# One fixed place for the high and low parts of all seven-block weight chunks

## The chip, the cores and the metric

The kernel runs on one core of a Trainium2 chip. The metric is the device time of one execution in microseconds; the kernel before takes 1150.22 us, the median of three runs from 1149.85 to 1150.63.

## The reference

A two-layer encoder trunk over 512 tokens of 1024 features, in float32. Each layer is attention followed by a squared-ReLU MLP, both with a residual sum. The part that matters here is the MLP, whose two weight matrices are 1024 x 4096 and 4096 x 1024:

```python
def sq_relu_mlp(h, w_up, w_down):
    u = jax.nn.relu(h @ w_up)
    return (u * u) @ w_down

h = h + sq_relu_mlp(rmsnorm(h, norm_ffn[layer]), ffn_w_up[layer], ffn_w_down[layer])
```

## The kernel before

All activations are held transposed, features on the 128 partitions and tokens along the free dimension. A float32 product is made of three TensorE matmuls on rounded parts: high weights by high activations, high weights by low activations, low weights by high activations. The weight part is the stationary operand (128 x 128, loaded by a weight load that the profile calls PEld), the activation part is the moving one.

Most of the two MLP products go through a seven-multiplication scheme for 2 x 2 blocks (class Seven). There a **seven-block chunk** is a 256 x 256 piece of the weight matrix. Four of its 128 x 128 blocks are loaded by one DMA on SP's queue (line 367), three sums of blocks are made beside them in place (lines 372 to 374, on POOL, or on DVE for a few chunks of the down product), and the seven blocks that are needed lie then in columns 128 to 1023 of a 1024-column tile, 896 columns in all. ACT copies these 896 columns into a rounded high part (tile whi, line 379) and DVE subtracts that from the source into a low part (tile wlo, line 380).

In Seven.run, TensorE takes a chunk's seven blocks one after the other; for each block it does three matmuls with 256 moving columns (lines 467, 468 and 469): high part by x[:, 0], high part by x[:, 1], low part by x[:, 0]. That is 21 matmuls and 21 weight loads a chunk. Four chunks and more accumulate in half banks of PSUM, which ACT and DVE then add up (lines 475 to 479). The moving tiles are those of pool "big" (Slot, named a), 1024 columns of 4 bytes, and what is read of them starts at column 0, 256, 512 or 768.

There are 164 such chunks, in four stretches: 52 in the up product of the first layer, 32 in its down product, and 52 and 28 in the second layer. Between the stretches TensorE does the rest of the products with 512 moving columns (lines 623 to 625, function mm3), attention and norms.

Buffers: three tiles for high parts, four for low parts, four raw tiles, beside which a chunk's raw data goes into a slot of the big pool where enough are free. A planner that runs ahead of the products (weights, begin, preload) sets the order: DMAs five chunks ahead, sums up to three, the copy and the subtraction two.

All these tiles (a, whi, wlo, raw) have 1024 columns, that is 4096 bytes in each partition, and in the built program each of them begins at the same remainder modulo 256 bytes. So the column at which a part begins inside its whi or wlo tile, modulo 64, says how far it stands from the moving tiles modulo 256 bytes. In the kernel before, places() chooses that column anew for each chunk: chunk i has its high part at column 8 * (i mod 16) and its low part at that place moved on by a table's entry for i div 16, again modulo 128 columns.

```python
a = i % 16
return 8 * a, 8 * ((a + (0, 1, 2, 4, 8, 3, 6, 12, 15, 14)[i // 16 % 10]) % 16)
```

Of the kernel before, what the change touches and what calls it, by code (L numbers as in the profile page):

```python
# [9 lines left out]
F32R = mybir.dt.float32r  # L10
# [8 lines left out]
P = 128  # L19
# [11 lines left out]
def f32(ap):  # L31
    return ap.bitcast(F32)
# [3 lines left out]
def encoder_kernel(ctx: ExitStack, tc: tile.TileContext, ins, out, dbg=None):  # L36
# [5 lines left out]
    wp = ctx.enter_context(tc.tile_pool(name="wp", bufs=3))  # L42
# [19 lines left out]
    def nm(s):  # L62
        cnt[0] += 1
        return f"{s}_{cnt[0]}"
# [204 lines left out]
    def rows(w, k0, nk):  # L269
        return w[k0 * P : (k0 + nk) * P, :].rearrange("(k p) n -> p k n", p=P)  # L270
# [16 lines left out]
    def begin(i):  # L287
        while begun[0] < len(loaded):
            make = asked[begun[0]][0]
            if make is summed_chunk and begun[0] > i + SUM:  # L290
                break
            if make in (summed_chunk, seven_chunk):
                next(loaded[begun[0]])
            begun[0] += 1
# [55 lines left out]
    SEVEN = [(0, 0), (2, 2), (4, 5), (3, 3), (5, 4), (6, 1), (1, 6)]  # L350

    reserve = [3]
    place = [0]

    def places():

        i = place[0]
        place[0] += 1
        a = i % 16
        return 8 * a, 8 * ((a + (0, 1, 2, 4, 8, 3, 6, 12, 15, 14)[i // 16 % 10]) % 16)  # L360

    def seven_chunk(w, k0, c0, eng=None):


        slot = Slot(F32) if len(free) > reserve[0] else None
        raw = slot.t if slot else wp.tile([P, 1024], F32, tag="raw", bufs=4, name=nm("raw"))
        SP.dma_start(raw[:, 0:512].rearrange("p (k n) -> p k n", k=2), rows(w, k0, 2)[:, :, c0 : c0 + 256])
        r = raw.rearrange("p (b n) -> p b n", n=P)
        yield
        held = (lambda z: z) if eng else tc.keep_in_program_order  # L370
        eng = eng or POOL
        held(eng.tensor_tensor(r[:, 6], r[:, 0], r[:, 1], op=ALU.subtract))  # L372
        held(eng.tensor_tensor(r[:, 4:6], r[:, 2:3].to_broadcast([P, 2, P]), r[:, 0:7:6], op=ALU.add))  # L373
        held(eng.tensor_tensor(r[:, 7], r[:, 3], r[:, 5], op=ALU.subtract))  # L374
        yield
        a, b = places()
        hi = wp.tile([P, 1024], F32R, tag="whi", name=nm("whi"))[:, a : a + 896]
        lo = wp.tile([P, 1024], F32R, tag="wlo", bufs=4, name=nm("wlo"))[:, b : b + 896]
        ACT.activation(hi, raw[:, 128:1024], AF.Copy)  # L379
        DVE.tensor_tensor(lo, raw[:, 128:1024], f32(hi), op=ALU.subtract)  # L380
        if slot:
            slot.free()
        yield hi, lo, []

    class Seven:
# [63 lines left out]
        def plan(self, w, c0, pairs=None):  # L449

            return [plan(w, pairs[kp] if pairs else 2 * kp, c0, DVE if pairs and c0 and kp in (2, 5) else None,
                         make=seven_chunk)
                    for kp in range(self.np)]
# [1684 lines left out]
```

## Time and profile before

| what | value |
|---|---|
| median of three runs | 1150.22 us |
| the profiled execution | 1149.85 us |
| its span, first to last instruction | 1148.1 us |
| mean granted TensorE clock over the span | 0.998 of full speed |
| TensorE matmuls in the trace | 7348 |
| of these on lines 467 to 469 | 3444 |

The profile is of one execution. Busy times of TensorE are modelled at their ends, since matmuls are pipelined; starts are as recorded. Windows are given in microseconds from the start of the span, as from:to. A row of the list of groups names the line, the engine, the operation, the tile written and those read, the shapes and the count, then busy time and mean duration. In a timeline row stand the start, the length, engine, line, operation and tiles, and in brackets for how long the engine was idle and what ended that.

### The profile page before, as it was taken

To read this page: it belongs to the slowest core of one execution; us is meant where nothing else is said; L and a number is where in the kernel's file an instruction comes from. 1 tells how busy PE (TensorE), PEld (TensorE's weight loads), DVE (VectorE), ACT (ScalarE), POOL (GpSimd) and SP (SyncE) were. 2 spreads that over 40 slices of the span, in tenths; PEclk is the share of its full clock that TensorE was granted. 3 is DMA by queue.
4 is the path that set the end of the run, shared out by engine and by line. 5 is a ranking of instruction groups with operands and counts; after the bars stand their busy time and mean duration, and the time that the engine had idled before them with its cause. 6 is when DMAs were issued, how large, how long until landed. Compare 5 with 4: busy or idle time off the path is not lost.

```text
span 1148.1 us, 20506 instructions
## 1 busy us (share of the span) xinstructions
PE 1138.1 (99%) x7348; PEld 1025.7 (89%) x7348; DVE 894.2 (78%) x1570; ACT 669.3 (58%) x1133; POOL 602.7 (52%) x722
## 2 busy tenths in 40 slices
PE   9999999999999999999999999999999999999997
PEld 8787888888899999899998998988889999989996
DVE  7887998988968777978775666667997777697874
ACT  6676785755346668534464556545553666773334
POOL 4456432327698993379432232231388889435740
PEclk9999999999999999999999999999999999999999
DMA  7322441222523235933585565333344232372332
GB/s 238 108 71 76 112 123 56 65 65 95 170 85 97 89 93 147 275 97 102 147 171 159 149 174 129 117 109 120 106 151 128 75 95 90 77 190 72 121 121 74
DMA packets 118325, 136.06 MB, mean 119 GB/s; under 512 B 9923, under 2 KB 99952, under 8 KB 118224
## 3 DMA queue, kind: packets, MB, share of 16 engines
q1 hardware_dynamic: 110736, 119.83, 34.4%
q0 software_dynamic: 7312, 14.83, 6.7%
q8 instruction: 58, 0.95, 0.4%
q14 instruction: 43, 0.35, 0.1%
q10 hardware_dynamic: 176, 0.10, 0.0%
HBM read 112.70 MB, written 6.29 MB: 104 GB/s over the span
## 4 chain that ended last, share of the span: by engine, by line
PE 92%; issue 3%; DVE 3%; ACT 1%; POOL 0%; DMA 0%; POOLq 0%; DVEq 0%; ACTq 0%
PE mm L623 9%; PE mm L624 8%; PE mm L625 8%; PE mm L468 4%; PE mm L467 4%; PE mm L469 4%; PE t L468 3%; PE t L469 3%; PE t L467 3%; PE s L1148 3%; PE o L1136 3%; PE s L467 2%; PE s L468 2%; PE s L469 2%; PE s L623 2%
## 5 line engine op out<-in xcount | busy, mean ns | idle before, releaser
L380 DVE TENSOR_TENSOR wlo<-a,whi 128x896 fp32r<-128x896 f32 x106 | 129.7, 1227 | 58.9 <-ACT whi L379 58.4
L623 PE MATMUL mm<-a,whi 128*128 128x512 f32 x428 | 172.7, 404 | 0.1
L624 PE MATMUL mm<-a,whi 128*128 128x512 f32 x428 | 167.9, 392 | 0.0
L625 PE MATMUL mm<-a,wlo 128*128 128x512 f32 x428 | 167.0, 391 | 0.0
L379 ACT ACTIVATE whi<-a 128x896 fp32r<-128x896 f32 x106 | 100.8, 951 | 111.8 <-PE s L468 28.5
L224 DVE TENSOR_TENSOR wlo<-raw,whi 128x1024 fp32r<-128x1024 f32 (+4 forms) x93 | 105.4, 1139 | 27.0 <-ACT whi L234 26.6
L234 ACT ACTIVATE whi<-raw 128x1024 fp32r<-128x1024 f32 (+3 forms) x96 | 88.2, 920 | 56.3 <-PE s L624 23.2
L468 PE MATMUL mm<-a,whi 128*128 128x256 f32 x430 | 120.8, 281 | 0.0
L469 PE MATMUL mm<-a,wlo 128*128 128x256 f32 x430 | 120.7, 281 | 0.0
L467 PE MATMUL mm<-a,whi 128*128 128x256 f32 x430 | 120.6, 281 | 0.0
L379 ACT ACTIVATE whi<-raw 128x896 fp32r<-128x896 f32 x58 | 55.1, 954 | 84.1 <-PE s L468 23.0
L373 POOL TENSOR_TENSOR a<-a 128x256 f32<-128x256 f32 x104 | 96.9, 932 | 8.2
L625 PEld LDWEIGHTS mm<-a,wlo 128*128 128x128 f32 x428 | 80.3, 188 | 17.1
L374 POOL TENSOR_TENSOR a<-a 128x128 f32<-128x128 f32 x104 | 90.5, 870 | 8.2
L1156 POOL TENSOR_SCALAR p<-p,ti 128x512 f32<-128x512 f32 x64 | 48.0, 751 | 88.4 <-DVE ti L1155 67.7
L623 PEld LDWEIGHTS mm<-a,whi 128*128 128x128 f32 x428 | 80.5, 188 | 15.5 <-issue 0.5
L624 PEld LDWEIGHTS mm<-a,whi 128*128 128x128 f32 x428 | 80.7, 189 | 13.5
L372 POOL TENSOR_TENSOR a<-a 128x128 f32<-128x128 f32 x104 | 77.2, 743 | 27.8 <-DMA a<-in_ffn_w_up_dram 23.1
L1785 POOL TENSOR_SCALAR p<-p,ti 128x256 f32<-128x256 f32 x64 | 35.6, 567 | 104.5 <-DVE ti L1784 91.6
L380 DVE TENSOR_TENSOR wlo<-raw,whi 128x896 fp32r<-128x896 f32 x58 | 71.0, 1235 | 24.6 <-ACT whi L379 24.5
L468 PE MATMUL t<-a,whi 128*128 128x256 f32 x312 | 87.5, 281 | 0.0
L469 PE MATMUL t<-a,wlo 128*128 128x256 f32 x312 | 87.5, 280 | 0.0
(449 smaller groups left out, 3618.8 us busy)
## 6 DMA issues: line engine op xcount, KB each, us to landing
a<-in_ffn_w_up_dram SPq DMA_DIRECT2D x102, 256.0 KB, 2.7
raw<-in_ffn_w_down_dram SPq DMA_DIRECT2D x34, 512.0 KB, 4.4
raw<-in_ffn_w_down_dram SPq DMA_DIRECT2D x56, 256.0 KB, 2.6
raw<-in_od_w_qkv_dram SPq DMA_DIRECT2D x64, 128.0 KB, 3.5
raw<-in_ffn_w_up_dram SPq DMA_DIRECT2D x12, 512.0 KB, 4.1
wlo<-in_ffn_w_down_dram POOLq DMA_DIRECT2D x12, 512.0 KB, 6.2
a<-a SPq DMA_DIRECT2D x17, 256.0 KB, 3.4
bx<-a SPq DMA_DIRECT2D x32, 128.0 KB, 5.4
```

The lines of the kernel that those rows point to most:

```text
L224: z = lambda: (eng or DVE).tensor_tensor(to, src, f32(high), op=ALU.subtract)
L234: ACT.activation(hi[:, 0:m], raw[:, 0:m], AF.Copy)
L373: held(eng.tensor_tensor(r[:, 4:6], r[:, 2:3].to_broadcast([P, 2, P]), r[:, 0:7:6], op=ALU.add))
L374: held(eng.tensor_tensor(r[:, 7], r[:, 3], r[:, 5], op=ALU.subtract))
L379: ACT.activation(hi, raw[:, 128:1024], AF.Copy)
L380: DVE.tensor_tensor(lo, raw[:, 128:1024], f32(hi), op=ALU.subtract)
L467: PE.matmul(o, wh, x[:, 0], start=kp == 0 and n in (0, 1, 3, 5), stop=False, skip_group_check=True)
L468: PE.matmul(o, wh, x[:, 1], start=False, stop=False, skip_group_check=True)
L469: PE.matmul(o, wl, x[:, 0], start=False, stop=kp == self.np - 1, skip_group_check=True)
L623: PE.matmul(o, wh, xh, start=first, stop=False)
L624: PE.matmul(o, wh, xl, start=False, stop=False)
L625: PE.matmul(o, wl, xh, start=False, stop=last)
```

## The change

The function places() and its counter go. Every high part and every low part begins at column 16 (64 bytes) of its tile, for all 164 chunks. What is loaded, summed, copied, subtracted and multiplied, in which order and on which engine, is the same row for row in both programs; the tiles lie at the same addresses. Behind the edit the lines of the file stand ten lower in number (line 467 becomes 457).

```diff
     reserve = [3]
-    place = [0]
-
-    def places():
-
-        i = place[0]
-        place[0] += 1
-        a = i % 16
-        return 8 * a, 8 * ((a + (0, 1, 2, 4, 8, 3, 6, 12, 15, 14)[i // 16 % 10]) % 16)
-
     def seven_chunk(w, k0, c0, eng=None):
...
         yield
-        a, b = places()
-        hi = wp.tile([P, 1024], F32R, tag="whi", name=nm("whi"))[:, a : a + 896]
-        lo = wp.tile([P, 1024], F32R, tag="wlo", bufs=4, name=nm("wlo"))[:, b : b + 896]
+        hi = wp.tile([P, 1024], F32R, tag="whi", name=nm("whi"))[:, 16:912]
+        lo = wp.tile([P, 1024], F32R, tag="wlo", bufs=4, name=nm("wlo"))[:, 16:912]
         ACT.activation(hi, raw[:, 128:1024], AF.Copy)
         DVE.tensor_tensor(lo, raw[:, 128:1024], f32(hi), op=ALU.subtract)
```

## The prediction

> **What bounds the kernel now.** I read the page's first and fourth parts first, then the groups of instructions, then the table by windows for the four stretches in which the changed tiles are used. The page: shares of the span by engine, the chain that ended last, and two of its groups (line, engine, operation, count, busy time, mean ns).
>
> ```profile
> PE 1138.1 (99%) x7348; PEld 1025.7 (89%) x7348; DVE 894.2 (78%) x1570; ACT 669.3 (58%) x1133; POOL 602.7 (52%) x722
> ...
> PE 92%; issue 3%; DVE 3%; ACT 1%; POOL 0%; DMA 0%; POOLq 0%; DVEq 0%; ACTq 0%
> ...
> L469 PE MATMUL mm<-a,wlo 128*128 128x256 f32 x430 | 120.7, 281 | 0.0
> ```
>
> TensorE is 99% busy and carries 92% of the chain, so a microsecond that its stream loses or gains is a microsecond of the end. The mean of 281 ns is no price for a matmul: ends are modelled and neighbours overlap. What a matmul costs is the distance from its start to the next one's start, and that I read from the timeline.
>
> The seven-block chunks run in four stretches. In each row: the stretch, its length, then busy time of PE, PEld, DVE, ACT and POOL with counts, the granted clock, the DMA share and GB/s.
>
> ```profile
> 318.47:447.38 128.91, 128.91 (x1093) 128.90 (x1092) 94.84 (x109) 83.93 (x104) 107.95 (x128) 1.00 0.30 86
> 490.92:570.37 79.45, 79.45 (x673) 79.45 (x672) 59.84 (x70) 34.05 (x40) 58.74 (x64) 1.00 0.36 115
> 872.70:1001.79 129.09, 129.09 (x1094) 129.09 (x1093) 94.67 (x108) 83.59 (x103) 106.99 (x127) 1.00 0.29 83
> 1045.32:1114.73 69.41, 69.41 (x590) 69.41 (x589) 54.58 (x66) 28.25 (x33) 44.82 (x51) 1.00 0.38 122
> sum 406.86, PE 406.86 PEld 406.85 DVE 303.94 ACT 229.82 POOL 318.51; mean PE 101.72 PEld 101.71 DVE 75.98 ACT 57.45 POOL 79.63
> ```
>
> PE is busy in all of each stretch at full clock, and so is its weight load. 52 + 32 + 52 + 28 = 164 chunks of 21 matmuls take 406.86 us, 2.481 us each, or 118.1 ns a matmul. No other engine is full: POOL, the nearest, has 107.95 of 128.91 us.
>
> **What the places of before already show.** The change puts nothing new on the chip: it takes one of the places that the kernel of before goes through in turn and keeps it. By places(), chunk i starts its high part at column 8·(i mod 16), and a table shifts the low part from it. Modulo 64 columns (256 bytes) both parts stand at column 16 in chunks 2, 10, 66, 74 and 162. Windows cut from the first matmul of one chunk to the first of the next (PE alone; the count is 21 and the two or three that overlap a window's edge), in this order chunks 0, 1, 2, 3, 10, 36, 66, 162, 53 and 61:
>
> ```profile
> 318.47:320.98 2.51, 2.51 (x22) 1.00 0.67 214
> 320.98:323.47 2.49, 2.49 (x24) 1.00 0.00 2
> 323.47:325.85 2.38, 2.38 (x23) 1.00 0.38 110
> 325.85:328.38 2.53, 2.53 (x24) 1.00 0.35 104
> 343.32:345.70 2.38, 2.38 (x23) 1.00 0.42 120
> 407.77:410.22 2.45, 2.45 (x23) 1.00 0.00 1
> 525.74:528.12 2.38, 2.38 (x23) 1.00 0.20 68
> 1109.82:1112.20 2.38, 2.38 (x23) 1.00 0.98 339
> 493.40:495.88 2.48, 2.48 (x24) 1.00 0.31 105
> 513.24:515.75 2.51, 2.51 (x23) 1.00 0.30 101
> ```
>
> Chunk 0 has both parts at column 0, chunk 1 both at 8, chunk 3 both at 24, chunk 36 (32, 48) was among the fastest of the other places, and chunks 53 and 61 both have (40, 8). The same 21 matmuls take between 2.38 and 2.53 us by place alone. The four rows with the new place say 2.38 whether the DMA share beside them is 0.20 or 0.98, in both layers and at both ends of the kernel. The timeline shows it matmul by matmul, at the border of chunks 2 and 3 (start, length, engine, line):
>
> ```profile
> 325.51 0.28 PE L467 MATMUL s<-a,whi 128*128 128x256 f32 x1
> 325.62 0.28 PE L468 MATMUL s<-a,whi 128*128 128x256 f32 x1
> 325.73 0.28 PE L469 MATMUL s<-a,wlo 128*128 128x256 f32 x1
> 325.85 0.28 PE L467 MATMUL mm<-a,whi 128*128 128x256 f32 x1
> 325.97 0.28 PE L468 MATMUL mm<-a,whi 128*128 128x256 f32 x1
> 326.09 0.28 PE L469 MATMUL mm<-a,wlo 128*128 128x256 f32 x1
> ```
>
> Three matmuls of chunk 2 start 0.34 us apart (325.51 to 325.85), 113.3 ns each; from the border on the step is 0.12. No engine is waited for in either; the stream itself runs at another pace.
>
> A rule of the Trainium skill speaks against this: "SBUF — State Buffer", section "Who interferes with whom", gives TensorE two read ports, one for the moving operand and one for weight loads, calls them independent, and says that PE never waits on anyone. By that rule the place of the weights could not matter and the sum would be zero; the rows 2.38 and 2.53 disagree with it.
>
> **The change part by part.** No instruction is added, removed or moved on any engine or queue, and every operation keeps its size: per chunk one ACT copy (L379), one DVE subtraction (L380), 21 matmuls and 21 weight loads. Only column offsets differ.
>
> The matmuls: 21 steps at 0.34 us per three are 2.38 us a chunk, and 164 of them 390.3 us against 406.86 now: **16.5 us less**. A first matmul behind another kind of work may be some ns slower; with four entries that is nothing.
>
> The copy and the subtraction write to another place. Line 379's and 380's own durations (ns, minimum, median, maximum) over all the places:
>
> ```profile
> L379 ACT ACTIVATE whi<-a x106: 935/954/962, 307.6 to 1052.9; 128x896 fp32r<-128x896 f32 x106
> L380 DVE TENSOR_TENSOR wlo<-a,whi x106: 1077/1174/1642, 311.6 to 1053.9; 128x896 fp32r<-128x896 f32 x106
> ```
>
> ACT differs by 27 ns at most; costed at nothing, since both engines are idle between chunks. L380's spread is wide, but where it is long POOL stands beside it, at whatever place. If ACT or DVE were slower by such an amount, it would be hidden by the lead below.
>
> What comes late next is preparation. TensorE will ask for a chunk 0.10 us sooner than for the one before it, so the sums, copy and subtraction of the last chunk of a long stretch (52) are wanted about 5 us sooner than now. Chunk 51, the last of the first stretch (its last sum on POOL, its copy on ACT, its first matmul), and, as one of the tightest low parts, chunk 153 (its subtraction and its first use):
>
> ```profile
> 434.28 1.32 POOL L374 TENSOR_TENSOR a<-a 128x128 f32<-128x128 f32 x1
> ...
> 440.12 0.95 ACT L379 ACTIVATE whi<-a 128x896 fp32r<-128x896 f32 x1
> ...
> 444.91 0.28 PE L467 MATMUL mm<-a,whi 128*128 128x256 f32 x1
> ...
> 1085.79 1.35 DVE L380 TENSOR_TENSOR wlo<-raw,whi 128x896 fp32r<-128x896 f32 x1
> ...
> 1087.72 0.28 PE L469 MATMUL s<-a,wlo 128*128 128x256 f32 x1
> ```
>
> POOL is done at 435.60, 4.5 us before ACT takes the chunk up; ACT is done at 441.07, 3.84 us before TensorE needs it. Together 8.3 us cover a shift of 51 × 0.10 = 5.1, if POOL keeps its pace; a longer stay of POOL behind a denser DVE would take some of the remaining 3. Chunk 153's low part is done 0.58 us before its use, because DVE is held by the evacuation of the group that ended two chunks earlier. That evacuation moves with TensorE, so only two chunks' worth of shift, 0.2 us, is lost and 0.38 stays. Nothing in the rows makes a wait certain; bounds are 0 and, from the ring below, 7.5 us; I take 0.5 us, near the zero that every stretch shows now, for one or two low parts that come late.
>
> Behind the first stretch lies one in which the transfers are dense:
>
> ```profile
> 447.40:490.90 43.50, 43.50 (x194) 36.02 (x193) 40.02 (x69) 27.29 (x42) 15.75 (x21) 1.00 0.91 254
> ```
>
> PE never idles there, though the DMA share is 0.91. It will begin 5 us sooner; so will its transfers, which are issued as tiles come free behind ACT and DVE work of the same stretch, so I cost it at nothing. If they did not move, up to those 5 us would be waited for here, which lies inside the range below.
>
> Sum against the profiled execution's own 1149.85 us (span 1148.1): 1149.85 − 16.5 + 0.5 = 1133.8. Its time is the lowest of the three runs shown, 0.37 under their median, so a median should come at **1134.2**.
>
> **The rivals.** *Preparation becomes the bound.* In the second stretch, where raw tiles are recycled, the timeline has a ring of three engines:
>
> ```profile
> 499.56 1.16 DVE L380 TENSOR_TENSOR wlo<-raw,whi 128x896 fp32r<-128x896 f32 x1 [1.34 <-ACT whi L379]
> 499.86 1.19 POOL L374 TENSOR_TENSOR raw<-raw 128x128 f32<-128x128 f32 x1
> ...
> 501.08 0.95 ACT L379 ACTIVATE whi<-raw 128x896 fp32r<-128x896 f32 x1 [1.55 <-POOL raw L374]
> ...
> 502.06 1.17 DVE L380 TENSOR_TENSOR wlo<-raw,whi 128x896 fp32r<-128x896 f32 x1 [1.34 <-ACT whi L379]
> ...
> 504.57 1.16 DVE L380 TENSOR_TENSOR wlo<-raw,whi 128x896 fp32r<-128x896 f32 x1 [1.34 <-ACT whi L379]
> ```
>
> and in the list of waits (in total, times, longest):
>
> ```profile
> ACT whi L379 <- POOL raw L374: 17.7, 11, 2.0
> ```
>
> POOL's last sum lies under DVE's subtraction until that ends, ACT waits for POOL and DVE for ACT; a turn takes 2.505 us (499.56 to 504.57 for two), longer than the new 2.38. If it held through both stretches with recycled raw tiles (32 + 28 chunks), 60 × 0.125 = 7.5 us would come back in place of the 0.5: 1134.2 + 7.0 = 1141.2; with the spare 3.8 us of each stretch used up first it gives nothing. For it: the ring is longer than the need. Against it: ACT waited for POOL's last sum of a raw tile 11 times among 60 chunks, some chunks' sums go to DVE there, and POOL has 58.74 busy us in 79.45. Its middle is 1137.5.
>
> *A slow pattern locks in.* The place alone does not set the pace: chunks 53 and 61 have the same one modulo 256 bytes and take 2.48 and 2.51. So the order in which loads and streams fall beside each other has more than one steady form. All chunks at the new place were entered from a chunk at column 8 (chunks 1, 9, 65, 73 and 161); the four stretches will be entered from other matmuls, and nothing would then shake the stream out. If it settles in the form of chunk 3, 164 × 2.53 = 414.9: 8.1 us more, 1158.3; it is a loss from 2.481 us a chunk on. Against it: in chunk 0, entered from another product, the 0.12 pace stood from the second matmul, as in its later twins, and all quoted fast chunks have one pace.
>
> *The place does nothing over a whole stretch*: the fast chunks would owe their pace to having just left another place, and in an even run loads and streams would not disturb each other otherwise than on average; 2.481 us a chunk stay, 1150.2. Against it: the 0.34 holds to the last three matmuls of chunk 2, and begins anew in each of the four rows. Two independent ports, as in the page of the Trainium skill named above ("SBUF — State Buffer"), would end here too.
>
> **How the numbers follow.** Forecast 0.81, preparation 0.12, slow pattern 0.04, no effect 0.03. The forecast's own spread is 1133 to 1136 (no wait at all, or 2 us of them); most of the preparation case is taken in: 1132.5 to 1139. About 0.2% (2.3 us) is what a measurement of this kernel can tell from no change; both the forecast and the preparation case are faster by more: faster 0.93, same 0.03, slower 0.04.
>
> **What would show it.** The four stretches cut in the same way should be about 124, 76, 124 and 67 us, and three matmuls of lines 467 to 469 (ten lines higher in the changed file) 0.34 us apart in all of them. If the stretches are longer, gaps in front of a chunk's first high or low matmul, with PE waiting for ACT's copy or DVE's subtraction, would speak for preparation; an even step of 0.12 for a slow pattern or none. The time between the stretches should stay as it is. I would be wrong most by an uneven pace inside a stretch that no row of before shows.

## The result and the profile after

The changed kernel takes 1148.07 us (median of 16 runs, 1146.44 to 1149.51) against 1149.79 us before (median of 16, 1149.19 to 1151.03): a ratio of 0.9982, 95% interval 0.9975 to 0.9990. That is 1.7 us less, where about 16 were forecast, and it lies outside the forecast range. The spread between executions grew from 1.8 to 3.1 us.

The profiled execution took 1147.28 us (span 1145.5). The four stretches, cut as before the change (columns: stretch, length, busy time of PE, PEld, DVE, ACT and POOL with counts, clock, DMA share, GB/s):

```profile
317.92:446.54 128.62, 128.62 (x1094) 128.61 (x1093) 96.32 (x109) 83.84 (x104) 103.57 (x127) 1.00 0.30 86
490.08:568.50 78.42, 77.67 (x674) 77.11 (x673) 62.03 (x72) 33.97 (x40) 59.02 (x66) 1.00 0.37 118
870.76:999.37 128.61, 128.61 (x1094) 128.61 (x1092) 95.58 (x108) 83.34 (x103) 105.79 (x127) 1.00 0.28 83
1042.94:1112.20 69.26, 69.26 (x590) 69.25 (x589) 54.87 (x66) 28.19 (x33) 44.78 (x51) 1.00 0.38 123
sum 404.91, PE 404.16 PEld 403.59 DVE 308.79 ACT 229.34 POOL 313.15; mean PE 101.04 PEld 100.90 DVE 77.20 ACT 57.33 POOL 78.29
```

The long stretches take 128.6 us, not 124: PE is busy all through them, at full clock, and nobody is waited for. Only the second stretch has PE idle time (78.42 less 77.67) and is shorter by 1.0 us. The timeline of the first stretch, with the line numbers of the changed file (457 to 459), shows an even step that is not the forecast one:

```profile
400.25 0.28 PE L457 MATMUL mm<-a,whi 128*128 128x256 f32 x1
400.37 0.28 PE L458 MATMUL mm<-a,whi 128*128 128x256 f32 x1
400.49 0.28 PE L459 MATMUL mm<-a,wlo 128*128 128x256 f32 x1
400.60 0.28 PE L457 MATMUL mm<-a,whi 128*128 128x256 f32 x1
```

Three matmuls take 0.35 us; over a whole chunk, start to start, it is 2.473 us or 117.8 ns a matmul, in all 52 chunks. In the second stretch the same program at the same place runs otherwise. Here is chunk 54, with DVE's subtractions (line 370) in between:

```profile
494.57 2.08 DVE L370 TENSOR_TENSOR wlo<-raw,whi 128x896 fp32r<-128x896 f32 x2
...
495.26 0.28 PE L457 MATMUL s<-a,whi 128*128 128x256 f32 x1
495.38 0.28 PE L458 MATMUL s<-a,whi 128*128 128x256 f32 x1
...
495.70 0.38 PE L459 MATMUL s<-a,wlo 128*128 128x256 f32 x1
495.93 0.28 PE L457 MATMUL t<-a,whi 128*128 128x256 f32 x1
496.04 0.28 PE L458 MATMUL t<-a,whi 128*128 128x256 f32 x1
496.15 0.28 PE L459 MATMUL t<-a,wlo 128*128 128x256 f32 x1
496.26 0.28 PE L457 MATMUL t<-a,whi 128*128 128x256 f32 x1
```

The first of the two subtractions, chunk 54's low part, is ready at about 495.65, late; the matmul that needs it starts at 495.70 instead of 495.50. Up to here the step was 0.12, also behind a like wait in chunk 53 (a step of 0.23); behind this wait it is 0.11, 113.3 ns on average, and stays so through chunk 78, past a step of 0.98 in chunk 63. At chunk 79 another late low part (a step of 0.19) ends it, and from chunk 80 on it is 117.8 again. So one place has **two steady paces**, and a wait can turn the stream from one to the other, though not every wait does.

By starts, the sum of the four stretches went from 406.86 to 404.89 us. With all chunks at 117.8 ns it would be 164 x 2.473 = 405.6; 23 chunks at 2.380 take off 2.1, and the waits of chunks 53, 54, 63 and 79, the longest a step of 0.98 us, put 1.5 back. The other 0.6 us of the profiled difference lie outside the stretches and within the spread of executions.

### The profile page after: what moved, and what is told of

The parts are those of the page before. It is cut to its first block, busy times and chain, and to the rows that moved or that the text cites. A ratio compares the mean times of both kernels' runs of the same rounds, so it can differ in the third digit from the quotient of the medians.

```text
span 1145.5 us, 20506 instructions
## 1 busy us (share of the span) xinstructions
PE 1134.6 (99%) x7348; PEld 1021.9 (89%) x7348; DVE 897.0 (78%) x1570; ACT 668.1 (58%) x1133; POOL 596.0 (52%) x722
## 4 chain that ended last, share of the span: by engine, by line
PE 90%; DVE 4%; issue 4%; ACT 1%; POOL 0%; DMA 0%; POOLq 0%; DVEq 0%; ACTq 0%
PE mm L613 9%; PE mm L614 8%; PE mm L615 8%; PE mm L459 4%; PE mm L458 4%; PE mm L457 4%; PE t L459 3%; PE t L458 3%; PE t L457 3%; PE s L1138 3%; PE o L1126 3%; PE s L459 2%; PE s L458 2%; PE s L457 2%; PE t L1113 2%
## 5 line engine op out<-in xcount | busy, mean ns | idle before, releaser
L370 DVE TENSOR_TENSOR wlo<-a,whi 128x896 fp32r<-128x896 f32 x106 | 132.7, 1255 | 54.1 <-ACT whi L369 53.8
L365 POOL TENSOR_TENSOR a<-a 128x128 f32<-128x128 f32 x104 | 97.1, 934 | 8.2
L364 POOL TENSOR_TENSOR a<-a 128x256 f32<-128x256 f32 x104 | 94.0, 904 | 8.1
L457 PE MATMUL t<-a,whi 128*128 128x256 f32 x312 | 87.5, 280 | 0.0
L458 PE MATMUL t<-a,whi 128*128 128x256 f32 x312 | 87.5, 280 | 0.0
```

The costliest lines, as they stand in the source:

```text
L457: PE.matmul(o, wh, x[:, 0], start=kp == 0 and n in (0, 1, 3, 5), stop=False, skip_group_check=True)
L458: PE.matmul(o, wh, x[:, 1], start=False, stop=False, skip_group_check=True)
```

## The experiments

Two theories stood against each other at first: that the beginning of a stream decides between two paces of one place (A), and that the fast pace of chunks 54 to 78 belongs to that part of the kernel (B). All paces below are distances between starts, averaged over a chunk's 21 matmuls, waits left out.

### Entering each stretch as chunks 0 to 2 did before

```diff
+        i, place[0] = place[0], place[0] + 1
+        a = {0: 0, 1: 8}.get(i - max(z for z in (0, 52, 84, 136) if z <= i), 16)
-        hi = wp.tile([P, 1024], F32R, tag="whi", name=nm("whi"))[:, 16:912]
-        lo = wp.tile([P, 1024], F32R, tag="wlo", bufs=4, name=nm("wlo"))[:, 16:912]
+        hi = wp.tile([P, 1024], F32R, tag="whi", name=nm("whi"))[:, a : a + 896]
+        lo = wp.tile([P, 1024], F32R, tag="wlo", bufs=4, name=nm("wlo"))[:, a : a + 896]
```

> Every stretch begins with one chunk at column 0 and one at column 8, as chunks 0 and 1 of the kernel before; all others stay at column 16. Theory A (a stream at column 16 has two steady paces, 113.3 and 117.8 ns a matmul; which one it takes is settled by how the stream falls into step at its beginning, and it is kept until a wait): from the third chunk on 113.3 ns, the two long stretches 50 x 2.380 + 2.51 + 2.49 = 124.0 us each instead of 128.6, the whole 1136 to 1140 us, and preparation begins to be waited for. Theory B (the fast pace of chunks 54 to 78 belongs to that part of the kernel, whose chunks are prepared in recycled raw tiles, and not to how the stream began): the long stretches stay at 128.6, the whole at about 1148 us.

Measured: 1143.21 us, ratio 0.9941 (0.9926 to 0.9956). Every stretch is at 113.3 ns from its third chunk on. The third stretch keeps it for all 50 chunks, past a late low part in chunk 102 (a step of 0.17), and takes 124.81 us; the step of 0.86 at its end is a wait of the product behind it for that product's own high part. The first loses it: low parts of chunks 17, 18, 19, 31 and 33 to 35 come late, and from chunk 36 on it runs at 117.8 to its end.

```profile
318.00:444.91 126.91, 126.91 (x1093) 126.23 (x1092) 98.46 (x109) 84.16 (x104) 108.14 (x128) 1.00 0.31 87
488.45:567.70 79.25, 78.61 (x673) 78.21 (x672) 61.76 (x70) 33.92 (x40) 56.21 (x64) 1.00 0.37 115
870.01:994.82 124.81, 124.23 (x1094) 124.03 (x1092) 96.83 (x108) 82.31 (x102) 105.09 (x128) 1.00 0.29 84
1039.28:1108.67 69.39, 68.19 (x589) 67.99 (x588) 56.08 (x66) 28.23 (x33) 44.92 (x51) 1.00 0.39 122
...
994.82 0.50 PE L616 MATMUL s<-a,whi 128*128 128x512 f32 x1 [0.58 <-ACT whi L234]
```

A holds and B falls: two chunks of another place at the beginning change the pace of the fifty behind them. It also shows the second part of the missing gain, preparation that comes late at the fast pace. What the steps at late low parts have beyond an even one (with chunks 63, 66 and 153 of the down stretches) adds up to 3.8 us, and behind such steps 43 chunks stand at 117.8 again, which is 4.0 us more. The whole is 3 us over the upper end of A's expectation. Chunk 153, which the prediction had looked at, in this run (lines 460 to 462 here, the subtraction is line 373, the sums on DVE lines 364 to 366, the evacuation of the group before lines 469 to 472):

```profile
1071.06 2.90 DVE L373 TENSOR_TENSOR wlo<-raw,whi 128x896 fp32r<-128x896 f32 x2
1073.87 0.67 DVE L469 TENSOR_TENSOR a<-a,mm 128x512 f32<-128x512 f32 x1
...
1077.16 0.84 DVE L364 TENSOR_TENSOR raw<-raw 128x128 f32<-128x128 f32 x1 [0.49 <-DMA raw<-in_ffn_w_down_dram]
1077.93 0.67 DVE L472 TENSOR_TENSOR a<-a,s 128x512 f32<-128x512 f32 x1
1078.52 0.41 DVE L365 TENSOR_TENSOR raw<-raw 128x256 f32<-128x256 f32 x1
1078.86 1.21 DVE L1595 TENSOR_TENSOR hT<-hT,a 128x1024 f32<-128x1024 f32 x1
1079.99 0.54 DVE L366 TENSOR_TENSOR raw<-raw 128x128 f32<-128x128 f32 x1
1080.46 2.62 DVE L373 TENSOR_TENSOR wlo<-raw,whi 128x896 fp32r<-128x896 f32 x2
...
1080.12 0.28 PE L461 MATMUL s<-a,whi 128*128 128x256 f32 x1
1081.59 0.38 PE L462 MATMUL s<-a,wlo 128*128 128x256 f32 x1 [1.20 <-DVE wlo L373]
```

In these rows the end of an evacuation (L472, L1595) and the sums of a later chunk, the first of which waited 0.49 us for a DMA, stand on DVE ahead of the subtraction, and the stream stops for 1.2 us.

### One chunk at column 8 in the middle

```diff
+        a = 8 if i in (26, 68, 110, 150) else 16
```

> All chunks at column 16 but one in each stretch (numbers 26, 68, 110 and 150), at column 8. Theory A: in the two long stretches 26 chunks at 2.474, one at about 2.485, then 25 at 2.380 us, 126.3 us instead of 128.6, with no wait at the change of pace; the whole 1141 to 1145 us. Theory B: no change of pace at that chunk, 128.6 us, about 1148 us.

Measured: 1146.86 us (one run). In the long stretches nothing changes, 117.8 ns before and behind the chunk (128.62 us each). Behind chunk 68 it is 113.3 ns to the end of its stretch; chunk 150 leaves 117.9, and the change to 113.3 comes at chunk 153, whose low part is done only 0.17 us before its use; no wait is shown there. So A's expectation, that a single chunk at column 8 always leads into the fast pace, failed; what the chunk does depends on how the stream reaches it.

### Every fourth chunk at column 8

```diff
+        a = 8 if i % 4 == 0 else 16
```

> Each fourth chunk at column 8, the three behind it at column 16, so that a stream that lost the fast pace gets a new beginning every 10 us. Theory A: 2.485 + 3 x 2.380 us for each four, 41 x 9.63 = 394.7 us in place of 404.9, the whole about 1138 us and up to 3 us more by waits. Theory B: 2.485 + 3 x 2.474, the whole about 1148.5 us.

Measured: 1146.29 us, ratio 0.9968 (0.9956 to 0.9981), 8 us over A's sum. The three chunks behind each column-8 chunk of the first stretch had these paces:

```
fours 1 to 6:   113.3  117.8  117.9  113.4  117.8  117.9   (and so on, in turn)
```

Without any wait the two long stretches go through the same cycle of three, fast, slow, slow. Each pace comes back within 0.2 ns, and which one comes goes with the one before: coming from 113.3, the column-8 chunk runs at 118.5 and leads to 117.8; coming from 117.8, it runs at 118.1 and leads to 117.9; coming from 117.9, it runs at 118.2 and leads to 113.4. The single chunks at column 8 of the run before fit this: chunk 26 was reached at 117.8, ran at 118.1 and led to 117.9, chunk 68 was reached at 117.9, ran at 118.2 and led to 113.4.

### The same place, another moment

One more matmul of 32 to 256 columns ahead of each group, on the group's own first two tiles; its result is overwritten. (The groups are of four chunks in the up products and of eight or seven in the down products, 34 in all.)

```diff
                     o = half(bk[i], z)
+                    if kp == 0 and n == 0:
+                        m = 32 * (1 + shift[0] % 8)
+                        shift[0] += 1
+                        PE.matmul(o[:, 0:m], wh, x[:, 0, 0:m], start=True, stop=False, skip_group_check=True)
```

> All chunks at column 16. In front of the first matmul of each group of four chunks one more matmul on the same two tiles is put, with 32, 64, ... 256 columns in turn, whose result the next one overwrites: the place is the same, and only the moment at which the stream goes on differs. It costs 0.03 to 0.11 us for each of 41 groups, some 3 us. Theory A: the pace changes at such a matmul from 117.8 to 113.3 ns or back without a wait of another engine, and differs between groups of one stretch; the whole 1140 to 1151 us. A rival of A, that a stream is fast only behind a chunk at another place or behind a wait: all groups of the long stretches stay at 117.8, the whole about 1151 us.

Measured: 1149.46 us (one run). Every chunk's place is column 16, and the groups of the first stretch run at

```
columns   32     64     96     128    160    192    224    256    32     64     96     128    160
ns        113.3  117.8  117.8  113.3  117.8  117.8  117.8  117.8  117.8  113.3  117.8  113.3  117.8
```

The timeline at the tenth of these groups (lines 462 to 464 are the three matmuls, 461 the extra one with 64 columns):

```profile
407.52 0.28 PE L462 MATMUL s<-a,whi 128*128 128x256 f32 x1
407.63 0.28 PE L463 MATMUL s<-a,whi 128*128 128x256 f32 x1
407.75 0.28 PE L464 MATMUL s<-a,wlo 128*128 128x256 f32 x1
407.87 0.19 PE L461 MATMUL s<-a,whi 128*128 128x64 f32 x1
407.90 0.36 PE L462 MATMUL s<-a,whi 128*128 128x256 f32 x1
408.10 0.28 PE L463 MATMUL s<-a,whi 128*128 128x256 f32 x1
408.22 0.28 PE L464 MATMUL s<-a,wlo 128*128 128x256 f32 x1
408.33 0.28 PE L462 MATMUL t<-a,whi 128*128 128x256 f32 x1
```

Ahead of it the step is 0.12, behind it the group's mean is 113.3 ns. No other engine is waited for at these changes and no tile lies elsewhere; but for the short matmul itself, with its weight load, only the moment differs. The short matmul alone does not explain the pace either: behind 32 columns the first group runs at 113.3 and the ninth at 117.8. The long stretches change pace seven times each in this way. That shows A, and the rival (another place or another engine's wait is needed) falls.

### The extra matmul at few places

```diff
+                        if shift[0] in (0, 13, 21, 34):
+                            PE.matmul(o[:, 0:32], wh, x[:, 0, 0:32], start=True, stop=False, skip_group_check=True)
+                        shift[0] += 1
```

> All chunks at column 16 as in the changed kernel; in front of the first matmul of each of the four stretches alone stands one more of 32 columns on the same tiles (four in all, some 0.1 us together). Theory A: the changed kernel's stream is at 117.8 ns only for the moment at which it began; with this other moment the long stretches begin at 113.3 ns and keep it until a wait, the whole 1141 to 1145 us. If instead the place before must be another one, the stretches stay at 117.8 ns and the whole at 1148 us.

With 34 groups these numbers are the beginnings of the first two stretches and chunk 100, amid the third; the fourth stretch has none. Measured: 1144.93 us (one run). The first two stretches begin at 113.3 ns. The third begins at 117.8 and turns to 113.3 at chunk 100, where the 32 columns stand, and the fourth is at 117.8 throughout. As A has it, with the fourth stretch for a comparison in the same run. The first loses the fast pace again at chunk 18, after late low parts (steps up to 0.32 us at 17 to 19).

### Relu and square behind the next copy

```diff
-                    if u in (14, 21, 24):
+                    if u in (21, 22, 24):
```

> As the run that enters each stretch by columns 0 and 8, and in the up product the relu and square of a finished group stand behind ACT's copy of the next chunk instead of ahead of it (steps 21, 22 and 24 in place of 14, 21 and 24). Theory P (the waits of chunks 17 to 19 and 31 to 35, the last of which lost the fast pace, come from that copy and with it DVE's subtraction standing behind ACT's 2.1 us of relu and square): those waits go, the first long stretch keeps 113.3 ns to its end and takes about 124.2 us instead of 126.9, the whole about 1140 us. Rival Q (DVE is too full in the fast pace whatever ACT's order): waits stay and the stretch is over 126 us, the whole 1142 to 1145 us.

Measured: 1146.27 us, ratio 0.9971 (0.9958 to 0.9984), slower than without the edit (on another chip). The waits at 17 to 19 went, but so did the fast pace ahead of them, and at 117.8 ns the changed kernel has no waits there either. The two DVE subtractions that follow the squares (line 1402) moved with them; chunk 15's low part now stands behind them and is late by some 0.05 us, and that is enough:

```profile
354.21 0.28 PE L461 MATMUL s<-a,whi 128*128 128x256 f32 x1
354.33 0.33 PE L462 MATMUL s<-a,wlo 128*128 128x256 f32 x1
354.49 0.28 PE L460 MATMUL t<-a,whi 128*128 128x256 f32 x1
354.61 0.28 PE L461 MATMUL t<-a,whi 128*128 128x256 f32 x1
354.73 0.28 PE L462 MATMUL t<-a,wlo 128*128 128x256 f32 x1
```

A step of 0.16 (354.33 to 354.49) once, and from chunk 16 to 51 the pace is 117.8; in the third stretch the same at chunk 99. In the fourth, chunk 153's low part comes later than before the edit (a step of 2.56 us), and the stretch takes 71.83 us in place of 69.39. P's forecast fails, and DVE's own queue holds low parts up here. Whether ACT's order was the cause at chunks 17 to 19 and 31 to 35 stays open, since the edit moved work of DVE too and the stream reached those chunks at the slower pace.

### Less work on DVE

```diff
             DVE.tensor_tensor(r[:, 0], r[:, 1], half(bk[2], 1), op=ALU.add)
-            DVE.tensor_tensor(r[:, 1:3], r[:, 1:3], two(bk[3]), op=ALU.add)
```

> As the run that enters each stretch by columns 0 and 8, with one DVE sum of 0.69 us left out of each group's evacuation (the last bank of the four is not added in, so that term is missing from the product). Theory R (what comes late at the fast pace is DVE: a low part stands behind the evacuation of the group before it, and the wait that follows throws the stream out of the fast pace): no low part of the long stretches comes late, both keep 113.3 ns and take 124.0 to 124.2 us (126.9 and 124.8 with the sum); the waits of chunks 63 and 153 shrink by about 0.7 us; the whole 1137 to 1141 us. If the waits of the long stretches stay, DVE's evacuation is not what holds the low parts up.

Measured: 1136.91 us (one run). The four stretches:

```profile
318.37:442.36 123.99, 123.99 (x1093) 123.99 (x1092) 88.69 (x96) 82.70 (x103) 110.67 (x131) 1.00 0.30 86
487.45:564.92 77.47, 77.26 (x673) 76.67 (x672) 60.58 (x69) 33.96 (x40) 59.26 (x65) 1.00 0.38 119
867.19:991.19 124.00, 124.00 (x1094) 123.99 (x1092) 90.30 (x96) 82.89 (x103) 108.91 (x128) 1.00 0.30 86
1034.93:1101.80 66.87, 66.87 (x589) 66.87 (x588) 51.53 (x63) 28.30 (x33) 47.74 (x51) 1.00 0.40 127
```

The long stretches keep 113.3 ns to the end without a wait, and so does the last. In the second, low parts still come late at chunks 54, 63 and 67 (steps of 0.31, 0.43 and 0.30; chunk 63's was 0.88 with the sum), and the pace stays at 113.3. POOL's and ACT's work is nearly as before; R holds for the long stretches. DVE is no more than 96.32 us busy in 128.62 in the changed kernel, yet in bursts behind a group it is the engine that is late.

### Entering again behind the waits

Two runs. The first has the later squares too, and pairs of chunks at columns 0 and 8 in the down stretches; the second has the order of before and pairs in all stretches.

```diff
+        a = 0 if i in (0, 52, 67, 84, 136, 155) else 8 if i in (1, 53, 68, 85, 137, 156) else 16
```

> As the first of this group, with a pair of chunks at columns 0 and 8 once more in each down stretch (chunks 67, 68 and 155, 156), behind the places where waits fell so far. Theory A: whatever pace the stream has there, it is 113.3 ns behind the pair; the down stretches take about 77.5 us (waits of about 1.2 included) and 68.3 us in place of 79.3 and 69.4, the whole 1136 to 1139 us. Against A: the pair leads into the slow pace when the stream was fast before it.

```diff
+        a = {0: 0, 1: 8}.get(i - max(z for z in (0, 20, 36, 52, 67, 84, 104, 120, 136, 155) if z <= i), 16)
```

> As the run that enters each stretch by columns 0 and 8, with such a pair once more at chunks 20, 36, 67, 104, 120 and 155, behind the places where low parts came late in it. A pair costs 2.51 + 2.49 - 2 x 2.38 = 0.24 us where the stream was fast, and turns it to 113.3 ns where it was slow. Theory A: behind every pair the pace is 113.3 ns, also where it was 117.8 ahead of it; 6 x 0.24 = 1.4 us are paid and some 40 chunks x 0.094 = 3.8 us won against the run without them, the whole 1140 to 1142 us median with less spread. If a pair can also lead into the slow pace, chunks behind some pairs stand at 117.8 and the whole is at 1143 us or over.

Measured: 1145.33 us, ratio 0.9947 (0.9927 to 0.9967), and 1142.24 us, ratio 0.9936 (0.9922 to 0.9950). Behind every pair the pace is 113.3 ns. Most pairs inside a stretch were reached at 113.3 already; only one, chunks 36 and 37 of the second run, was reached at 117.7, and behind it stands one step of 0.114 and then one more late low part before the even 113.3 from chunk 39 on. That a pair turns a slow stream inside a stretch rests on that one step. The first run misses its sum because the later squares cost the long stretches the fast pace at chunks 15 and 99, and chunk 153's low part made a step of 2.46 us. Behind that step the granted clock (the third figure from the right) was 0.50 for 3.4 us, and 13 steps took 0.21 us each, which is some 1.3 us more:

```profile
1083.90:1087.30 3.40, 3.33 (x15) 0.50 0.46 149
```

The second run misses by little: its low parts still come late at thirteen chunks, with steps up to 1.36 us. It is faster than the kernel before and than the changed one, but not clear of the run with pairs at the entries alone (0.9926 to 0.9956), and it varies between executions as much (1140.95 to 1144.69).

### Other places

```diff
-        hi = wp.tile([P, 1024], F32R, tag="whi", name=nm("whi"))[:, 16:912]
-        lo = wp.tile([P, 1024], F32R, tag="wlo", bufs=4, name=nm("wlo"))[:, 16:912]
+        hi = wp.tile([P, 1024], F32R, tag="whi", name=nm("whi"))[:, 48:944]
+        lo = wp.tile([P, 1024], F32R, tag="wlo", bufs=4, name=nm("wlo"))[:, 32:928]
```

> All high parts at column 48, all low parts at 32, which in the kernel before took 2.449 us a chunk in each of its five chunks (102, 110, 150, 158 and their like), entered from four other places. If this place has one pace only, 164 x 2.449 = 401.6 us in place of 406.9, the whole about 1144.6 us, without new waits and with little spread between executions. If it too has more than one, most of the stretches stand at another pace than 116.6 ns.

Measured: 1144.49 us, ratio 0.9951 (0.9936 to 0.9966), 1143.19 to 1145.10. All four stretches run at 115.6 ns, below the 116.6 of single chunks before, and stay there behind waits (steps of up to 0.98 us). By the function places(), the kernel before has four such chunks and not five, and modulo 64 columns all four were entered from one place, (40, 24): here too the rows held a single way in. Then the same place with the extra matmuls ahead of each group:

> Parts at columns 48 and 32, with the extra matmul of 32 to 256 columns ahead of each group as at column 16. Theory: this place has one pace, so behind each of the 34 extra matmuls it is 115.6 ns again within a chunk; the whole about 1144.5 + 3 us. If this place has two paces as column 16 has, some groups run at another, for all of their length.

Measured: 1152.93 us (one run). The theory falls. Of the thirteen groups of the first stretch eleven come back to 115.6 ns within one to three chunks, but behind 256 columns the pace is 117.8 for the whole group, and the next one, with 32, keeps it; seven of all 34 groups run so for their whole length, and an eighth until a late low part at chunk 153. This place has a second pace as well, and in the plain run above nothing led into it.

The last run gave each four chunks a place of their own, 41 fours on the way through the kernel.

```diff
+        g, place[0] = place[0] // 4, place[0] + 1
+        a, b = (16, 48, 32, 56, 0, 48)[g // 8], 8 * (g % 8) if g < 40 else 32
```

> The place changes every four chunks: high parts at 16, 48, 32, 56 and 0, and for each of these the low parts at 0, 8, ... 56. If the place settles the pace after a short beginning, each four chunks end at one pace of their own, and the pairs (48, 32), (32, 48), (16, 48) settle at 115 to 117 ns as in single chunks of before, no pair under 113.3. If the way in matters at other places as it does at column 16, the pair (48, 32), which comes twice, and pairs that stood in before can show other paces than there. No forecast of the whole but 1145 to 1152 us.

Measured: 1148.73 us (one run). Paces of the last of each four, in ns (rows: column of the high part; columns: of the low part):

```
        0      8     16     24     32     40     48     56
16   117.8  117.9  113.3  119.0  118.5  117.8  113.3  117.0
48   117.8  117.8  119.0  117.8  115.6  117.6  117.8  117.8
32   118.3  117.8  118.9  120.0  118.6  117.8  116.5  120.0
56   117.7  117.8  119.2  119.0  117.8  117.8  117.7  116.8
 0   120.0  118.2  117.8  119.0  119.4  117.7  117.8  117.8
```

No pair is under 113.3. 117.8 (within 0.1) stands at nearly half of the places, and it is the second pace of both that were looked at more closely, (16, 16) and (48, 32). The pair (16, 48) stood at 113.3 here in all its four chunks and at 116.7 in its single chunks before (2.451 us), so (16, 16) isn't alone in having more than one pace.

## Why the prediction was wrong

**The step that failed** is the first term of the sum: "21 steps at 0.34 us per three are 2.38 us a chunk, and 164 of them 390.3 us". The 2.38 was read correctly, five times out of five, and taken for a property of the place. It is one of two paces of that place. All five chunks had been entered from a chunk at column 8 that had itself been entered from column 0, and the five times were one case, not five. Entered from another product, as each of the four stretches is, the stream settled at 2.473 us, which is the old mean of 2.481 almost exactly; so most of the change's gain was not lost to another engine, it never came. Of the 16.5 us that the term promised, 3.4 came: 164 chunks at 2.473 us are 1.3 us less than before, and 23 chunks at 2.380 take off 2.1 more. The pairs at columns 0 and 8, the 32 extra columns at the beginning of a stretch and the shifted groups show this from three sides.

**The rival that was right** is the slow pattern that locks in. It had its evidence (two chunks at one place with 2.48 and 2.51, against the prediction's own "by place alone") and its condition ("will be entered from other matmuls, and nothing would then shake the stream out"), and got 0.04. What spoke against it there, that chunk 0 had the 0.12 pace of its later twins from the second matmul on, shows that column 0 finds one pace from several beginnings; it says nothing of column 16. Its price was also taken wrongly, from another place (2.53), so that it stood as a loss; the pace in which the stream did lock in was seen at no chunk at column 16 before, and on the average of all places it is nearly neutral. With the chance put where the single way in would have it, near one half, the range would have reached up to 1150.

**The fast pace's worth** was sized rightly. With DVE relieved of one sum a group, the stretches take 123.99, 77.47, 124.00 and 66.87 us, against "about 124, 76, 124 and 67", and the whole 1136.91 against 1149.35 us on the same chip; the term left out of that kernel is 0.69 us of DVE work a group, no TensorE work.

**Preparation** was under-sized. Its 0.5 us was meant for low parts that come late; they cost 1.5 us in the changed kernel itself, at a pace little faster than before, and 3.8 us in the run entered by columns 0 and 8. The prediction held that chunk 153's low part, 0.58 us ahead of its use, would keep 0.38, since the evacuation ahead of it moves with TensorE. In the run entered by columns 0 and 8 it came 1.20 us too late, on two accounts. The kernel before begins that evacuation 7.5 us ahead of the matmul that uses the low part (1087.72):

```profile
1080.23 0.68 DVE L476 TENSOR_TENSOR a<-a,mm 128x512 f32<-128x512 f32 x1
```

In that run it began at 1073.87, 6.4 us ahead of the moment at which that matmul was due (0.11 us behind the one at 1080.12), right behind two subtractions of 2.90 us together. And from the beginning of the evacuation to that of the subtraction it took 6.6 us in place of 5.6, with the wait for a DMA and with sums of 0.84 and 0.54 us that take 0.29 each in the kernel before. Such subtractions of 896 columns take 1.08 to 1.10 us where POOL does nothing beside them; all that take over 1.3 us, 51 of 164 before and 69 in this run, have work of POOL beside them. That POOL stretches them is likely and was not tried. The waits also cost what the prediction had no term for: a wait of 0.05 us can put the stream back at 117.8 for the rest of its stretch, 36 chunks or 3.4 us in the run with the later squares.

**The places' part** stands: in one run, four chunks each, the table has paces from 113.3 to 120.0 ns with no other engine waited for. Each place but (48, 32) has one way in there, so a figure of the table is a pace of its place and need not be the only one; but column 16 settled at 113.3 or 117.8 and at nothing else in all the runs above. The rule of the Trainium skill ("SBUF — State Buffer", section "Who interferes with whom"), by which TensorE's two read ports are independent and PE never waits, does not agree with that table. By the prediction's reading it forecast no change, and 0.9982 is near that; but this does not bear it out, for the same place entered another way gave 0.9941, and the pace that the stream fell into, 117.8 ns, merely lies near the mean of the places that it replaced, 118.1. Whether it is reads of loads and of moving tiles that disturb each other, no run here shows.

**The transfers** behind the first stretch were no bound, as predicted. With that stretch at its shortest (123.99 us) the second begins 45.1 us after the end of the first (442.36 to 487.45) instead of 43.5, so 1.6 us are given back there. The window between them, the only wait of TensorE in it that another engine ends, and the subtraction that it waits for (line 617 there is a matmul of 512 columns, line 224 the subtraction for its low part):

```profile
442.36:487.45 45.09, 43.85 (x195) 35.96 (x193) 40.91 (x67) 28.49 (x43) 15.01 (x21) 1.00 0.93 253
```

```profile
444.24 0.50 PE L617 MATMUL s<-a,wlo 128*128 128x512 f32 x1 [1.24 <-DVE wlo L224]
...
441.86 2.32 DVE L224 TENSOR_TENSOR wlo<-raw,whi 128x1024 fp32r<-128x1024 f32 x1 [4.25 <-ACT whi L234]
```

45.09 less 43.85 is this one wait of 1.24 us, and again a subtraction is late, not a DMA: it begins when ACT's copy is done, and it takes 2.32 us, where in the kernel before it takes 1.23:

```profile
445.84 1.23 DVE L224 TENSOR_TENSOR wlo<-raw,whi 128x1024 fp32r<-128x1024 f32 x1 [3.16 <-ACT whi L234]
```

Two copies on POOL (lines 1498 and 1499) run beside it here and not in the kernel before. It does not take an earlier end of the stretch: in the run with the short matmul ahead of each group the first stretch ends at 447.19 (447.38 before), the same two copies fall beside a subtraction of 2.33 us, and the part behind it takes 44.9 us. In the run entered by columns 0 and 8 that part takes 43.54 us (444.91 to 488.45), as before, but behind the third stretch, from where the next product was due (994.08) to the fourth (1039.28), the same run takes 45.2 us in place of 43.5, 1.1 of them in waits for ACT's high part (shown above) and DVE's low part.

What stays open is what in the chip makes the two paces, and why 117.8 ns comes at so many places. Runs can tell how a stream gets into a pace, not what keeps it there. Nor was it tried to take DVE's bursts away in a kernel that computes everything.

## What to carry to other kernels

A pace seen in the middle of a mixed stream belongs to that stream's way in as much as to its operands; before a gain is multiplied over a kernel, the rows must hold more than one way in, and the number of independent ones counts, not the number of rows. An evenly running TensorE stream of weight loads and matmuls may be some per cent off its best without any wait in the profile, and a chunk or two at another place, or a small matmul ahead of it, can set it right: here two chunks a stretch took the kernel from 0.9982 to 0.9941 of the time before; more pairs behind the known waits, at 0.9936, are not clear of that. Each engine's queue needs its own look for what comes late: the shares of busy time had DVE at 74% in the long stretches, and with one of its sums a group left out their waits were gone.

## What the runs showed of the hardware that was not expected

- Two steady paces for the same instructions at the same addresses, 113.3 and 117.8 ns for 256 moving columns with a weight load each, both at full granted clock; kept for up to 52 chunks (1092 matmuls), and left, in these runs, at a wait, an extra matmul or a change of place, and once (chunk 153 of the run with single chunks at column 8) at a low part that was done 0.17 us before its use, with no wait shown.
- A wait of about 0.05 us (a step of 0.16 instead of 0.11) was enough to change the pace, while another of that size (a step of 0.17 at chunk 102 of the run entered by columns 0 and 8) and waits of 0.9 us left it as it was.
- Behind stops of TensorE with steps of 2.46 and 2.56 us (chunk 153 of the two runs with the later squares) the granted clock was 0.50 for 3.4 us; behind steps of up to 1.64 us inside the kernel it stayed at 1.00.
- Executions of these programs differ more: 1146.4 to 1149.5 us for the changed kernel (16 runs), 1141.8 to 1145.4 with the pairs at the entries (4 runs), against 1149.2 to 1151.0 before (16 runs), whose places change with each chunk. That the two paces are the reason is likely, but only one execution of each has a trace.
